# Stick-breaking attention: the transposes of two tiles at every other step, in place of one tile at each

## The chip, the core and the metric

The kernel runs on one NeuronCore of one Trainium2 chip. The metric is the device time of one execution in microseconds. A core has TensorE (PE, with its weight loads shown as PEld), VectorE (DVE), ScalarE (ACT), GpSimd (POOL) and SyncE (SP, which issues the DMAs). Each of them works through its own instructions in the order in which the program gives them, and waits on semaphores for what another engine has to finish first.

## What is computed

One layer (`DEPTH = 1`) over 2048 tokens of width 1024: modulated RMSNorm, a stick-breaking attention with 16 heads of 64, an output projection, and a SwiGLU network of width 2816. Only the attention is touched by the change. Cut to that:

```
z = q k^T * 64**-0.5                       # per head, s_pos < t_pos only
rest = reverse cumulative sum over s of softplus(z)
a = exp(z - rest)                          # 0 where s_pos >= t_pos
o = a v
```

The kernel uses exp(z - rest) = sigmoid(z) times the product of sigmoid(-z) over all later positions. So a row of `a` is a sigmoid times a running product, and the running product is a scan from the right.

## The kernel before

**Units and steps.** The attention is cut into 160 units: 8 pairs of heads (`p`), 4 blocks of 512 queries (`qb`), 2 heads of the pair (`e`), and the blocks of 512 keys from the diagonal one back to the first (`sc`). A unit has four tiles of 128 queries by 512 keys, called rows `r`; on the diagonal row `r` has only `(r + 1) * 128` keys. The main loop (L1020) runs over 640 steps `s` and some more to drain; step `s` begins tile `s`, which is row `s % 4` of unit `s // 4`. Further stages of older tiles are done in the same step, with a delay in steps. All four computing engines take their instructions in the order of the source (`manual_schedule`); nothing is reordered by a planner. This list (L56) is therefore the order of every queue:

```
ORDER_IN_SLOT = [
    ("av", 9), ("score", 0), ("proj", 0), ("turn", 6), ("sig", 0), ("stick", 0), ("high", 6), ("low", 6)
]
```

**The stages.** `score` (L501) is two matmuls into one of two PSUM banks of the pool `zps`. `sig` is two sigmoids on ACT: `a` = sigmoid(z) into SBUF (L518) and sigmoid(-z) back into the same PSUM bank (L520). `stick` is a scan on DVE (L535, on the diagonal L530) that reads that bank, and a product on POOL (L542) that completes the tile of weights `a`. Since a scan is the last reader of its bank, the scores of step `s` can only begin when the scan of step `s - 2` has ended. `turn` (L552) transposes 128 keys of all four rows of a unit, so four transposes on PE (one to four on the diagonal), into one of the two PSUM banks of the pool `tps`. `high` (L562, ACT) and `low` (L568, DVE) split that bank into two tiles of the reduced format fp32r, rounded value and remainder; after `low` the bank is free. `av` (L580) is two matmuls that add the weighed values of those 128 keys.

**The projections beside it.** `proj` puts slices of the coming projections of q, k and v between the others, by `project_to`: about 1.3 slices a step, a slice being three matmuls (`mm3`, L144 to L146), so most steps have one, some two, some none. Where a product is complete, ACT copies it (L404 for k and q, L443 for v) and DVE takes the remainder (L405). For v two slices are left empty (`VGAP = 2`) and then PE turns the copy (L449), which ACT and DVE split again (L453, L454). In the first pair of heads `proj` also turns the normed input (L297, `x_turn`), in the same two banks of `tps`. From step 120 on, at every even step (`LATE_FROM, LATE_STEP = 120, 2`), one piece of the modulation vectors is added up on DVE (L204).

Of the kernel before, what the change touches and what calls it, by code (L numbers as in the profile page):

```python
# [52 lines left out]
    "tmp": 4, "w": 3, "a": 10,  # L53
}

ORDER_IN_SLOT = [  # L56
    ("av", 9), ("score", 0), ("proj", 0), ("turn", 6), ("sig", 0), ("stick", 0), ("high", 6), ("low", 6)
]

LATE_FROM, LATE_STEP = 120, 2  # L60
# [19 lines left out]
def hybrid_trunk_kernel(  # L80
# [401 lines left out]
    def project_to(n):  # L482

        nonlocal done
        while done < min(n, sum(SLICES)):
            next(pending)
            done += 1
        if done == sum(SLICES):
            next(pending, None)
# [425 lines left out]
    def wo_load(half, k2, tag):  # L915
        hl = att.tile([P, 2, 2, BT], F32R, name=f"wo{half}_{k2}", tag=tag, bufs=BUFS[tag])
        nc.sync.dma_start(f32(hl), wo_s[half][:, 2 * k2 : 2 * k2 + 2])
        w_o[half, 2 * k2], w_o[half, 2 * k2 + 1] = hl[:, 0], hl[:, 1]

    def lead_in(first, end):  # L920

        for n in range(first, end + 3):
            if n < end:
                o_load(0, n)
            if first <= n - 2 < end:
                o_add(0, n - 2)
            if first <= n - 3 < end:
                o_prep(0, n - 3)
            yield

    def gate_load(which, tiles):
        for half, sl in enumerate(HALVES):
            tiles.append(att.tile([P, BT], F32, name=f"gate{which}_{half}", tag="w", bufs=BUFS["w"]))
            nc.sync.dma_start(tiles[half], gate_rows[which, :, sl])

    def out_projection(b):


        tiles = [(i, half) for i in range(4) for half in range(2)]
        if b in (0, NB - 1):  # L940
            tiles.sort(key=lambda t: t[1])
        for at, (i, half) in enumerate(tiles):
            y_ps[b, i, half] = bank("x", at % (4 if b else 2), f"y{b}_{i}_{half}")
            for k in range(KC):
                ts = slice(i * P, (i + 1) * P)
                mm3(
                    y_ps[b, i, half], (o_split[b, k][:, 0, ts], o_split[b, k][:, 1, ts]),
                    (w_o[half, k][:, 0], w_o[half, k][:, 1]), k == 0, k == KC - 1,
                )
                tick()  # L950
                beside_out(b, 8 * at + k)
                yield
            after(1, y_square, b, i, half)
            if half == 0:
                continue
            if b == 0:
                after(1, y_gate, i)
            after(2, y_norm, b, i)

            held = LAST_HELD if (b, i) == (NB - 1, 3) else 0  # L960
            after(7 + held, x1_add, b, i)
            after(10 + held, x1_square, b, i)
            after(16 + held, x1_scale, b, i)
        for k in range(KC):
            after(19 + held + H2_STEP * k, h2_turn, b, k)
# [44 lines left out]
        "score": score, "sig": sigmoids, "stick": break_sticks,  # L1010
        "turn": turn, "high": split_high, "low": split_low, "av": weigh_values,
    }
    last = max(d for _, d in ORDER_IN_SLOT)
    weight = 0.0
    wo_weights = split_wo()
    ahead_of_wo = lead_in(0, 6)
# [3 lines left out]
    for s in range(4 * len(units) + last):  # L1020
        if s % 4 == 0 and s // 4 < len(units):
            p, e, qb, sc = units[s // 4]
            at = STEPS.index((p, qb)) if (p, qb) != PARKED else STEPS.index((p, 1)) - 1
            project_to(sum(SLICES[: at + 1]) + 1)
        if s >= LATE_FROM and s % LATE_STEP == 0:
            next(late, None)
        if s >= SPLIT_FROM and s % SPLIT_STEP == 0:
            next(wo_weights, None)
        if s >= lead_from and s % WO_STEP == 0:
            next(ahead_of_wo, None)  # L1030
        if done == sum(SLICES):
            if first_out is None:
                first_out = out_projection(0)
                for k2, tag in enumerate(("ht", "ht", "ht", "ht")):
                    wo_load(1, k2, tag)
                for step in ahead_of_wo:
                    pass
                ahead_of_wo = lead_in(6, KC)
            elif s < 4 * len(units):
                next(ahead_of_wo, None)  # L1040
            if s == 4 * len(units):
                gate_load(0, gate)
            if s >= 4 * len(units) - OUT_BEFORE:
                for _ in range(1 if s < 4 * len(units) else 3):
                    next(first_out, None)
        for stage, delay in ORDER_IN_SLOT:
            if stage == "proj":
                i = min(s // 4, len(units) - 1)
                weight += DIAG_WEIGHT if units[i][2] == units[i][3] else 1.0
                project_to(AHEAD - max(0, EAGER - 1 - s) + weight * RATE)  # L1050
            elif 0 <= s - delay < 4 * len(units):
                stages[stage](*divmod(s - delay, 4))
# [489 lines left out]
```

## Time and profile before

| | us |
|---|---|
| median of 3 runs | 2930.34 |
| lowest, highest | 2928.61, 2930.91 |
| the profiled execution | 2927.62 |
| its span in the profile | 2925.8 |
| PE busy | 2842.0 (97%) |
| DVE busy | 2059.7 (70%) |
| ACT busy | 1651.9 (56%) |
| POOL busy | 1264.7 (43%) |

The span is the profiled execution from its first to its last instruction; 1.8 us of the execution lie outside it. That execution is 2.7 us shorter than the median of the runs. An engine's busy time is the union of its instructions' times; a matmul's end is modelled, so consecutive matmuls overlap in the records and a PE that is shown busy may still have waited for a short while. The attention steps lie between 90 and 1460 us of the span; the output projection and the SwiGLU network follow.

### The profile page before, as it was taken

The numbers are of one execution on the slowest core, as the hardware profiler recorded it, in microseconds if no ns is written. First come the engines' busy times: TensorE is split into PE (matmuls) and PEld (weight loads), VectorE is DVE, ScalarE is ACT, GpSimd is POOL, SyncE is SP. The second block draws the span as 40 slices with busy tenths as digits, with TensorE's granted clock in tenths as the row PEclk, the third lists the DMA queues.
The fourth block names the chain that finished last, engine by engine and source line by source line (L and its number), as shares of the span: only waits on it lengthen the run. The fifth ranks groups of instructions, "written<-read, shape, count | busy, mean of one in ns | idle before, by whom it ended". The sixth has DMA issues, their size and how long they took to land.

```text
span 2925.8 us, 41798 instructions
## 1 busy us (share of the span) xinstructions
PE 2842.0 (97%) x13840; PEld 2323.1 (79%) x13840; DVE 2059.7 (70%) x2828; ACT 1651.9 (56%) x3265; POOL 1264.7 (43%) x2024
## 2 busy tenths in 40 slices
PE   7999999999999999999999999999999999999998
PEld 5788887788877888887887788888778888888886
DVE  5788898888888888889865756555675555233477
ACT  4787877777787777777644533333433333322243
POOL 0465666566575655655410122212222222644454
PEclk9999999999999999999999999999999999999999
DMA  8765647657565545646288644335453335545565
GB/s 298 276 204 168 188 142 229 198 164 232 163 212 195 185 133 169 202 121 229 63 294 294 212 137 152 108 95 158 135 182 103 93 103 170 187 139 154 181 219 179
DMA packets 237481, 516.85 MB, mean 177 GB/s; under 512 B 22224, under 2 KB 108240, under 8 KB 219344
## 3 DMA queue, kind: packets, MB, share of 16 engines
q1 hardware_dynamic: 237264, 514.18, 54.8%
q8 instruction: 109, 1.79, 0.2%
q14 instruction: 108, 0.88, 0.1%
HBM read 346.85 MB, written 118.49 MB: 159 GB/s over the span
## 4 chain that ended last, share of the span: by engine, by line
PE 78%; DVE 8%; issue 4%; ACT 4%; DMA 3%; POOL 2%; SPq 0%; DVEq 0%; POOLq 0%; ACTq 0%
PE s L144 9%; PE s L145 9%; PE s L146 9%; PE z L501 8%; PE o L580 7%; PE t L552 7%; PE pj L144 5%; PE pj L145 5%; PE pj L146 5%; PE o L144 4%; PE o L146 4%; PE o L145 4%; DVE w L535 2%; PE y L144 1%; PE y L146 1%
## 5 line engine op out<-in xcount | busy, mean ns | idle before, releaser
L542 POOL TENSOR_TENSOR a<-a,w 128x512 f32<-128x512 f32 (+3 forms) x640 | 617.7, 965 | 232.9 <-DVE w L535 143.0
L535 DVE TENSOR_TENSOR_SCAN w<-z,c,begin 128x512 f32<-128x512 f32 x384 | 491.1, 1279 | 88.8 <-ACT z L520 65.5
L144 PE MATMUL s<-r,l 128*128 128x512 f32 x1232 | 486.5, 395 | 12.6 <-DVE p L1313 10.2
L145 PE MATMUL s<-r,l 128*128 128x512 f32 x1232 | 483.7, 393 | 0.0
L146 PE MATMUL s<-r,l 128*128 128x512 f32 x1232 | 483.3, 392 | 0.0
L518 ACT ACTIVATE a<-z 128x512 f32<-128x512 f32 (+3 forms) x640 | 344.5, 538 | 145.0 <-PE z L501 121.3
L580 PE MATMUL o<-aT,v 128*128 128x512 f32 (+3 forms) x1280 | 412.4, 403 | 0.0
L562 ACT CAST aT<-t 128x512 fp32r<-128x512 f32 (+3 forms) x640 | 337.9, 528 | 124.6 <-PE t L552 116.6
L568 DVE TENSOR_TENSOR aT<-t,aT 128x512 fp32r<-128x512 f32 (+3 forms) x640 | 376.6, 588 | 26.5 <-ACT aT L562 25.6
L501 PE MATMUL z<-kt,qt 128*128 128x512 f32 (+3 forms) x1280 | 370.1, 370 | 23.9 <-DVE w L535 13.3
L552 PE MATMUL t<-begin,a 128*128 128x128 f32 x2176 | 342.2, 272 | 3.1 <-DVE aT L568 2.7
L520 ACT ACTIVATE z<-z 128x512 f32<-128x512 f32 (+3 forms) x640 | 342.6, 535 | 0.0
L552 PEld LDWEIGHTS t<-begin,a 128*128 128x128 f32 x2176 | 272.9, 140 | 86.9 <-DVE aT L568 6.1
L1321 POOL TENSOR_TENSOR one<-p,p 128x512 f32<-128x512 f32 x44 | 70.8, 1610 | 609.0 <-issue 307.2
L144 PE MATMUL pj<-ht,w 128*128 128x512 f32 x768 | 313.0, 408 | 10.6 <-ACT ht L671 5.7
L145 PE MATMUL pj<-ht,w 128*128 128x512 f32 x768 | 306.1, 399 | 0.4 <-DVE ht L676 0.4
L146 PE MATMUL pj<-ht,w 128*128 128x512 f32 x768 | 304.4, 396 | 0.0
L501 PEld LDWEIGHTS z<-kt,qt 128*128 128x128 f32 x1280 | 225.0, 188 | 86.4 <-DVE w L535 29.3
L144 PEld LDWEIGHTS s<-r,l 128*128 128x128 f32 x1232 | 232.5, 189 | 67.0 <-DVE p L1313 6.3
L146 PEld LDWEIGHTS s<-r,l 128*128 128x128 f32 x1232 | 232.5, 189 | 51.3
L145 PEld LDWEIGHTS s<-r,l 128*128 128x128 f32 x1232 | 232.6, 189 | 50.4 <-issue 0.5
L530 DVE TENSOR_TENSOR_SCAN w<-z,begin 128x128 f32<-128x128 f32 (+3 forms) x256 | 209.7, 819 | 79.8 <-ACT z L520 66.7
(156 smaller groups left out, 4872.5 us busy)
## 6 DMA issues: line engine op xcount, KB each, us to landing
ht<-h_s SPq DMA_DIRECT2D x108, 1024.0 KB, 8.2
wi<-in_win SPq DMA_DIRECT2D x86, 512.0 KB, 4.0
qt<-qn SPq DMA_DIRECT2D x124, 256.0 KB, 4.5
ol_qt<-act_s SPq DMA_DIRECT2D x56, 512.0 KB, 3.7
act_s<-S SPq DMA_DIRECT2D x66, 256.0 KB, 4.0
br<-in_wout SPq DMA_DIRECT2D x66, 256.0 KB, 3.6
h_s<-ht SPq DMA_DIRECT2D x16, 1024.0 KB, 8.3
o_s<-os SPq DMA_DIRECT2D x128, 128.0 KB, 2.4
```

Of the source, the lines that this page charges most:

```text
L144: nc.tensor.matmul(acc, lhs[0], rhs[0], start=first, stop=False, **kw)
L145: nc.tensor.matmul(acc, lhs[0], rhs[1], start=False, stop=False, **kw)
L146: nc.tensor.matmul(acc, lhs[1], rhs[0], start=False, stop=last, **kw)
L501: nc.tensor.matmul(z[:, :n], q[:, e, part, r * P : (r + 1) * P], k[:, e, :n], start=part == 0, stop=part == 1,)
L518: nc.scalar.activation(a[:, :n], z[:, :n], AF.Sigmoid, scale=QK_SCALE)
L520: nc.scalar.activation(z[:, :n], z[:, :n], AF.Sigmoid, scale=-QK_SCALE)
L535: nc.vector.tensor_tensor_scan(rest[:, rev], left[:, rev], begin[:, :BT][:, rev], initial=carries[r], op0=ALU.mult, op1=ALU.bypass,)
L542: nc.gpsimd.tensor_tensor(a[:, :n], a[:, :n], rest[:, 1 : n + 1], op=ALU.mult)
L552: nc.tensor.transpose(pt[:, rb * P : (rb + 1) * P], weighed[i, rb][:, j * P : (j + 1) * P], ident)
L562: nc.scalar.copy(hl[:, 0, t0:], pt[:, t0:])
L568: nc.vector.tensor_tensor(hl[:, 1, t0:], pt[:, t0:], f32(hl[:, 0, t0:]), op=ALU.subtract)
L580: nc.tensor.matmul(acc[:, t0:], lhs, hl[:, part, t0:], start=sc == qb and j == 0 and part == 0, stop=sc == 0 and j == 3 and part == 1,)
```

## The change

The list becomes two lists, one for even and one for odd steps. At an even step `s` the tiles `s - 6` and `s - 5` are both transposed, at an odd step none is. The splits keep their delay of 6, but at an odd step `high` and `low` stand ahead of `sig` and `stick`, so that the second bank of a pair is split in the step after its transposes before that step's sigmoids and scan.

```diff
 ORDER_IN_SLOT = [
-    ("av", 9), ("score", 0), ("proj", 0), ("turn", 6), ("sig", 0), ("stick", 0), ("high", 6), ("low", 6)
+    [("av", 9), ("score", 0), ("proj", 0), ("turn", 6), ("turn", 5),
+     ("sig", 0), ("stick", 0), ("high", 6), ("low", 6)],
+    [("av", 9), ("score", 0), ("proj", 0), ("high", 6), ("low", 6), ("sig", 0), ("stick", 0)],
 ]
...
-    last = max(d for _, d in ORDER_IN_SLOT)
+    last = max(d for order in ORDER_IN_SLOT for _, d in order)
...
-        for stage, delay in ORDER_IN_SLOT:
+        for stage, delay in ORDER_IN_SLOT[s % 2]:
```

## The prediction

> **What bounds it now.** I read the page first, then the stretch of the attention, its waits, and the timelines of single engines. Busy times, and the shares of the chain that ended last:
>
> ```profile
> PE 2842.0 (97%) x13840; PEld 2323.1 (79%) x13840; DVE 2059.7 (70%) x2828; ACT 1651.9 (56%) x3265; POOL 1264.7 (43%) x2024
> PE 78%; DVE 8%; issue 4%; ACT 4%; DMA 3%; POOL 2%; SPq 0%; DVEq 0%; POOLq 0%; ACTq 0%
> ```
>
> TensorE bounds the whole. The stretch of the attention alone:
>
> ```profile
> core 0: us, PE busy (x) PEld busy (x) DVE busy (x) ACT busy (x) POOL busy (x), PEclk, DMA share, GB/s
> 90.00:1460.00 1370.00, 1336.16 (x7223) 1093.46 (x7222) 1164.13 (x1495) 1058.84 (x2190) 822.35 (x1715) 1.00 0.56 181
> ```
>
> DVE is busy 1164.13 of 1370 us (85%), so PE leads by little. The waits there (who waited for whom: us in total, times, longest):
>
> ```profile
> ACT aT L562 <- PE t L552: 116.6, 223, 2.4
> DVE w L530 <- ACT z L520: 66.7, 110, 1.9
> DVE w L535 <- ACT z L520: 65.5, 159, 1.9
> PEld z L501 <- DVE w L535: 29.3, 49, 1.7
> ```
>
> ACT and DVE wait often, PE seldom, and then for a scan that frees a bank of scores. Ends of matmuls being modelled, I counted PE's stalls from starts: a pair of score matmuls that begins later than its predecessor's usual spacing allows. From step 24 on they sum to 38.0 us: 23.8 us in 41 even steps, 14.2 us in 26 odd ones. A change of order can win little more; the matmuls remain. Two steps and a stall, PE first (start, duration):
>
> ```profile
> 1234.26 0.71 PE L580 MATMUL o<-aT,v 128*128 128x512 f32 x2
> 1234.80 0.62 PE L501 MATMUL z<-kt,qt 128*128 128x512 f32 x2
> 1235.26 0.39 PE L144 MATMUL pj<-ht,w 128*128 128x512 f32 x1
> 1235.49 0.40 PE L145 MATMUL pj<-ht,w 128*128 128x512 f32 x1
> 1235.73 0.40 PE L146 MATMUL pj<-ht,w 128*128 128x512 f32 x1
> 1235.96 0.60 PE L552 MATMUL t<-begin,a 128*128 128x128 f32 x4
> 1236.32 0.71 PE L580 MATMUL o<-aT,v 128*128 128x512 f32 x2
> 1236.86 0.63 PE L501 MATMUL z<-kt,qt 128*128 128x512 f32 x2
> 1237.33 0.60 PE L552 MATMUL t<-begin,a 128*128 128x128 f32 x4
> 1237.68 0.71 PE L580 MATMUL o<-aT,v 128*128 128x512 f32 x2
> 1239.18 0.44 PE L501 MATMUL z<-kt,qt 128*128 128x128 f32 x2 [0.79 <-DVE w L535]
> ```
>
> ACT at the same place:
>
> ```profile
> 1236.16 0.59 ACT L443 COPY vT<-pj 128x512 f32<-128x512 f32 x1 [1.04 <-PE pj L146]
> ```
>
> and DVE, in brackets the idle time before an instruction and who ended it:
>
> ```profile
> 1234.65 1.28 DVE L535 TENSOR_TENSOR_SCAN w<-z,c,begin 128x512 f32<-128x512 f32 x1 [0.19 <-ACT z L520]
> 1235.85 0.67 DVE L568 TENSOR_TENSOR aT<-t,aT 128x512 fp32r<-128x512 f32 x1
> 1237.84 1.28 DVE L535 TENSOR_TENSOR_SCAN w<-z,c,begin 128x512 f32<-128x512 f32 x1 [1.33 <-ACT z L520]
> ```
>
> A full step with one slice lasts 2.06 us (1234.26 to 1236.32). In the next one the slice is empty, and the copy of v, which waits on ACT for the product of its own step, has held the sigmoids behind it for 1.04 us; so the scan is late and PE stands.
>
> **The transposes on PE.** No instruction is added or removed. Transposes in a row begin 109 ns apart (807 pairs, 700 to 1400 us). Behind a group, the first `o` begins 28 ns after the last transpose, but the second comes 316 ns later, in place of 233: 28 + 83 = 111, so leaving the transposes costs about nothing. Eight in a row also appear: four `vt` at 101.51, four `xT` at 101.95, 0.44 us for four. Turning eight at once saves 2 ns a pair, 0.6 us in 320 pairs.
>
> The granted clock is 1.00 over the stretch, in which transposes take 0.44 of every 2.06 us. The Trainium skill, "TensorE: Matmul & The Clock Gate" (Part 4: PE-mode transpose), holds that transposes do not count as activity for the clock gate like matmuls do, which speaks against bunching them; by it some windows could lose clock. No run so far shows it.
>
> **The order on ACT and DVE, pair by pair.** From the timelines: a scan ends 3.19 us after its scores begin (1232.74 to 1235.93) and starts 1.91 after; DVE is free for the next instruction 1.20 after a scan's start and 0.60 after a `low`'s. Let an even step's scores begin at 0, full tiles, one slice a step. Before: scan 1.91 to 3.19; `low` from 3.11, DVE free at 3.71; the odd scores begin at 2.06, their scan is ready at 3.97: 0.26 us to spare in every step. Scores two steps on are due at 4.12, the bank was free at 3.24: 0.88 of reserve. After: eight transposes shift the odd scores by 0.36 to 2.42. Scan 1.91 to 3.19, two `low` until 4.31, odd scan ready at 4.33, 0.02 to spare; DVE free at 5.53, the next even scan ready at 6.03, 0.50 to spare. Reserves for the scores: 0.88 and 0.88. So in a regular pair nothing moves. The 116.6 us that ACT waits for transposes may shrink, but no one on the path waits for that.
>
> What changes is where an extra DVE instruction falls.
> - Ahead of an even scan (the pieces of L204, 1.04 us each, are always there) it meets 0.50 of slack in place of 0.26: the scan is 0.24 earlier. Some 15 of the even stalls have it directly ahead: -3.6 us.
> - Ahead of an odd pair (remainders of k, q, v) the slack is 0.02 in place of 0.26. About 8 odd stalls: +1.9 us.
> - The ACT queue of an odd step becomes proj's copy, `high`, sigmoids. Where that copy waits for a matmul of its own step (12 turns of v and 8 product ends fall in odd steps), `high`, which had long been ready, is stuck behind it and the sigmoids come 0.50 later (one `high`). Where the bank's reserve is 0.5 or less, PE pays: 7 such places, at most +3.5 us. Queued behind are the sigmoids, scan and POOL product of that step; the scores two steps on wait.
>
> **The two banks of the transposes.** The second group of a pair needs the bank that the odd step before has already split: some 1.8 us early. In the first pair of heads three even-step groups wait for `low` now (2.7 us); with `low` ahead of the odd scan that wait goes: -2.7. But an `x_turn` at an odd step (four of them) now finds both banks taken and waits for the `low` of the even step before: between 0 and 1.8 us each, I take 2.5 us in all, since light steps are among them. The later uses, `av` three steps behind and POOL's product three steps ahead, keep over 3 us. No DMA moves.
>
> Sum: -3.6 + 1.9 + 3.5 - 2.7 + 2.5 - 0.6 = +1.0 us on 2927.6 for the profiled execution; against the median, which is 2.7 higher, 2931.
>
> **Rivals.**
> - *Slower, the odd scan last in its pair.* Both `low` stand ahead of it, 0.60 more, and only 0.36 is returned by later scores. A scan that is 0.24 later costs some 8 us over the odd steps' reserves (sum of what exceeds each); 0.44 later, 18 us; the full 0.61, 32. It decides once DVE is behind by more than those 0.02 us, which the 85% makes common; against it, a stalled PE gives the next pair its time back. With the ACT queue's 0.50 in addition, about 2945. A rule would have it so: the same page of the Trainium skill (table of the engine's figures) calls ScalarE's queue strictly first in, first out; the trace agrees in the 1.04 us row above.
> - *Faster, the even scan first.* If every even stall shrinks by 0.24 rather than only those behind L204, 41 x 0.24 = 9.8 and the three bank waits 2.7: 2918. At 0.61 each it would be some 18 + 2.7, 2909. For it: even steps hold 23.8 of the 38.0 us. Against: under a DVE backlog the work ahead of an even scan is the same in both orders.
> - *It does not do what it says:* the second group waits for its bank in most pairs, so PE stands with both groups and the order is only a delay. 320 x 0.1 us = 32 us, 2963; the 1.8 us of lead speak against it.
> - *The clock:* if it fell to half for one tenth of the attention, 137 us more. The granted 1.00 with 21% of transposes speaks against it.
>
> **How the numbers follow.** About 0.2% (5.9 us) can be told from no change. No change 0.42; odd scan slower 0.31; banks 0.02; clock 0.01; faster 0.24. The likeliest case's own range is 2925 to 2936. For 8 in 10 the range goes from 2914, most of the faster case, to 2949, the odd scan 0.44 later; about 0.08 lies below and 0.12 above.
>
> **What would show it.** Right: eight `t` in a row 109 ns apart, PE's busy time unchanged in the attention, ACT's wait for `t` below 116.6, stalls of `z` near 38 us with fewer on even steps, odd scans with next to no idle ahead of them. Wrong: the `z` stalls of odd steps well above 14 us (slower), of even steps well below 24 (faster), a wait of `t` for `aT` in most pairs, or a granted clock below 1.00.

## Result: 2925.86 us after, 2930.55 us before

| | before | after |
|---|---|---|
| median of 20 runs, us | 2930.55 | 2925.86 |
| lowest to highest, us | 2927.06 to 2932.63 | 2920.70 to 2927.93 |
| ratio to before, 95% interval | | 0.9984, 0.9977 to 0.9990 |
| profiled execution (its span), us | 2927.62 (2925.8) | 2925.50 (2923.7) |
| span from the first scores to the first product of the SwiGLU network, us | 1528.4 | 1524.7 |

The kernel became 4.7 us faster, 0.16%. The bound of 0.2% that the prediction took for what can be told from no change was too wide: with 20 runs a side the interval is clear of 1. The first scores begin at 93.5 us of the span after and at 91.2 before, a difference of the start that the other profiles show too (91.2 to 95.6 over all kernels); from there on the attention and the output projection take 3.7 us less.

Page and windows of the changed kernel; the columns are those of before:

```profile
PE 2841.5 (97%) x13840; PEld 2339.6 (80%) x13840; DVE 2035.9 (70%) x2828; ACT 1637.6 (56%) x3265; POOL 1269.3 (43%) x2024
PE 81%; DVE 7%; ACT 4%; issue 3%; DMA 3%; POOL 2%; SPq 0%; DVEq 0%; POOLq 0%; ACTq 0%
...
90.00:1460.00 1370.00, 1336.94 (x7238) 1110.72 (x7237) 1145.09 (x1498) 1046.88 (x2196) 827.52 (x1717) 1.00 0.56 182
```

PE's work is the same. DVE's is not: 2035.9 us against 2059.7, 19 us less in the attention alone, with the same 2828 instructions. That is the line to stop at, since nothing was taken from DVE. The waits in the attention:

```profile
DVE w L538 <- ACT z L523: 75.0, 147, 2.0
DVE w L533 <- ACT z L523: 66.6, 105, 1.9
ACT aT L565 <- PE t L555: 66.3, 138, 2.4
...
PEld z L504 <- DVE w L538: 26.4, 43, 1.4
```

ACT's wait for transposes fell from 116.6 to 66.3 us, as expected, and nobody gained by that. PE at the place that the prediction showed (lines are 3 further down in this kernel):

```profile
1234.02 0.63 PE L583 MATMUL o<-aT,v 128*128 128x512 f32 x2
1234.49 0.63 PE L504 MATMUL z<-kt,qt 128*128 128x512 f32 x2
1234.96 0.40 PE L147 MATMUL pj<-ht,w 128*128 128x512 f32 x1
1235.19 0.39 PE L148 MATMUL pj<-ht,w 128*128 128x512 f32 x1
1235.42 0.40 PE L149 MATMUL pj<-ht,w 128*128 128x512 f32 x1
1235.66 1.04 PE L555 MATMUL t<-begin,a 128*128 128x128 f32 x8
1236.45 0.72 PE L583 MATMUL o<-aT,v 128*128 128x512 f32 x2
1237.01 0.62 PE L504 MATMUL z<-kt,qt 128*128 128x512 f32 x2
1237.47 0.63 PE L583 MATMUL o<-aT,v 128*128 128x512 f32 x2
1238.88 0.44 PE L504 MATMUL z<-kt,qt 128*128 128x128 f32 x2 [0.78 <-DVE w L538]
```

Eight transposes in a row take 0.79 us to the next start, 0.36 before for four and 0.43 for the four more: 109 ns each, as worked out. The stall behind the copy of v is still there (0.78 against 0.79).

PE's stalls, counted from starts as in the prediction (delays under 60 ns left out, hence 37.5 for its 38.0):

| us | before | after |
|---|---|---|
| scores, even steps from 24 | 23.4 | 14.5 |
| scores, odd steps from 24 | 14.1 | 13.0 |
| transposes `t`, from step 24 | 1.1 | 7.2 |
| steps 0 to 23: scores; `t`; `xT` | 5.2; 3.5; 2.0 | 5.8; 0.6; 5.5 |
| projections and the rest | 9.5 | 8.6 |
| sum | 58.8 | 55.2 |

Of the 8.9 us that the even steps gained, 7.4 lie in steps 120 to 420 (16.3 to 8.9), where the late modulation is summed.

### The profile page after: what moved, and what is told of

It is laid out like the page before. It is cut to its first block, busy times and chain, and to the rows that moved or that the text cites. A ratio compares the mean times of both kernels' runs of the same rounds, so it can differ in the third digit from the quotient of the medians.

```text
span 2923.7 us, 41817 instructions
## 1 busy us (share of the span) xinstructions
PE 2841.5 (97%) x13840; PEld 2339.6 (80%) x13840; DVE 2035.9 (70%) x2828; ACT 1637.6 (56%) x3265; POOL 1269.3 (43%) x2024
## 4 chain that ended last, share of the span: by engine, by line
PE 81%; DVE 7%; ACT 4%; issue 3%; DMA 3%; POOL 2%; SPq 0%; DVEq 0%; POOLq 0%; ACTq 0%
PE s L147 9%; PE s L148 9%; PE s L149 9%; PE z L504 8%; PE o L583 7%; PE t L555 7%; PE pj L147 5%; PE pj L148 5%; PE pj L149 5%; PE o L148 4%; PE o L147 4%; PE o L149 4%; DVE w L538 2%; PE y L147 1%; PE y L148 1%
## 5 line engine op out<-in xcount | busy, mean ns | idle before, releaser
L583 PE MATMUL o<-aT,v 128*128 128x512 f32 (+3 forms) x1280 | 388.3, 385 | 0.0
L571 DVE TENSOR_TENSOR aT<-t,aT 128x512 fp32r<-128x512 f32 (+3 forms) x640 | 359.7, 596 | 25.3 <-ACT aT L565 24.9
L565 ACT CAST aT<-t 128x512 fp32r<-128x512 f32 (+3 forms) x640 | 313.2, 531 | 76.2 <-PE t L555 66.3
L555 PE MATMUL t<-begin,a 128*128 128x128 f32 x2176 | 292.3, 273 | 5.6 <-DVE aT L571 5.2
L555 PEld LDWEIGHTS t<-begin,a 128*128 128x128 f32 x2176 | 256.1, 140 | 51.3 <-DVE aT L571 6.9
L504 PEld LDWEIGHTS z<-kt,qt 128*128 128x128 f32 x1280 | 225.8, 188 | 77.5 <-DVE w L538 26.4
```

The source lines that it names most:

```text
L504: nc.tensor.matmul(z[:, :n], q[:, e, part, r * P : (r + 1) * P], k[:, e, :n], start=part == 0, stop=part == 1,)
L555: nc.tensor.transpose(pt[:, rb * P : (rb + 1) * P], weighed[i, rb][:, j * P : (j + 1) * P], ident)
L565: nc.scalar.copy(hl[:, 0, t0:], pt[:, t0:])
L571: nc.vector.tensor_tensor(hl[:, 1, t0:], pt[:, t0:], f32(hl[:, 0, t0:]), op=ALU.subtract)
L583: nc.tensor.matmul(acc[:, t0:], lhs, hl[:, part, t0:], start=sc == qb and j == 0 and part == 0, stop=sc == 0 and j == 3 and part == 1,)
```

## Experiments

Ratios are to the kernel before on the same chip. Three questions: which half of the change works, what the pieces of the modulation sums have to do with it, and what holds the transposes up.

### Which half works: pairs alone, early split alone

**x1_pairs_only**

```diff
-    [("av", 9), ("score", 0), ("proj", 0), ("high", 6), ("low", 6), ("sig", 0), ("stick", 0)],
+    [("av", 9), ("score", 0), ("proj", 0), ("sig", 0), ("stick", 0), ("high", 6), ("low", 6)],
```

> Pairs at even steps as in the change, but odd steps keep the old order (sigmoids and scan ahead of high and low). Queue theory: DVE's order is then that of before (scan, low, scan, low), and the second group of a pair waits for a low that comes last in the odd step: odd scores to scan end 3.19 us less 0.08 of overlap, low 0.67, four transposes 0.44, av 0.46 make a loop of about 4.7 us a pair against 4.1 to 4.5 now, so 40 to 170 us slower, about 3000 us, with some 0.2 to 0.5 us of wait of t for aT in most of the 320 pairs. Rival, that the pairing itself is what TensorE gains by (fewer changes between transposes and products): as fast as the changed kernel or faster, 2926 us or less.

Measured: 3057.78 us, 1.0436 (1.0421 to 1.0450), 129 us slower. In the waits of its attention (90 to 1580 us):

```profile
PEld t L555 <- DVE aT L571: 149.7, 181, 2.7
```

The second group of a pair waits for a `low` that comes last in the odd step. So TensorE gains nothing by the pairs as such; they need the split to go ahead.

**x2_lead_only**: one list for all steps.

```diff
+    [("av", 9), ("score", 0), ("proj", 0), ("turn", 5), ("high", 6), ("low", 6), ("sig", 0), ("stick", 0)],
```

> No pairs: one tile is turned at every step, with delay 5, and split a step later ahead of that step's sigmoids and scan (the odd order of the change at all steps). Queue theory: DVE alternates scan and low as before, each scan has the old 0.26 us to spare, so pieces of the modulation sums delay even scans as before: even stalls of z stay near 23 us; the waits of t for a bank (4.6 us before, 7.8 in the changed kernel) go to under 1, and the copies of proj that hold up high and sigmoids act in both parities. Together 2925 to 2933 us, between the two kernels. Rival, that the early split is the gain: 2925 or less with even stalls of 15 us or less. Rival, that the pairing is the gain: 2930 or more.

Measured: 2932.57 us, 1.0010 (1.0002 to 1.0019): inside the range, but not between the two kernels. It is slightly slower than the kernel before, where the second rival had put it. The stalls of scores fell, from 37.5 to 26.4 us, which I had not expected; and the waits of `t`, which I had put under 1 us, rose from 4.6 to 17.7 (steps 0 to 23 included). The early split moves waits from the scores to the transposes. So neither half gains alone. Two things were therefore open: why the scores wait less, and why the transposes wait.

### The pieces of the modulation sums

**x3_after_late_odd** and **x4_before_late_odd**: the same edit in the changed kernel and in the one before.

```diff
-        if s >= LATE_FROM and s % LATE_STEP == 0:
+        if s >= LATE_FROM and s % LATE_STEP == 1:
```

> The changed kernel, with the pieces of the late modulation sums (1.04 us each on DVE) put at odd steps in place of even ones. Queue theory: a piece now stands ahead of two lows and the odd scan, which has 0.02 us to spare in place of 0.50: the gain in steps 120 to 420 is lost, stalls of z there go back from 14.7 us to 20 or more, and the time to 2929 to 2933. Rival, that the gain has nothing to do with these pieces: 2926, stalls unchanged within 2 us.

> The kernel before, with the same pieces at odd steps. Queue theory: all steps have the same 0.26 us there, so the parity is nearly indifferent: within 3 us of the kernel before, 2927.5 to 2933.5. If the parity matters in itself (the pieces collide with other even-step work), it is faster by the 4 to 5 us of the change, 2926.

Measured: x3 2943.72 us, 1.0048 (1.0035 to 1.0061); x4 2937.53, 1.0032 (1.0021 to 1.0042). The gain of the change turned into a loss, by more than I gave it; and the kernel before lost too, which I had excluded. In both, two long waits of a product (`pj`) for its bank, of 1.7 to 2.2 us, came in at steps 173 and 376, with a window of half clock behind each (last section). They came with the new place of the pieces, so the pair is not clean: of x3's 19 us over the changed kernel, and of x4's 9 over the kernel before, some 6 are that. This is an estimate: the two waits, less the 1.4 us that stood at step 376 already, and 1.7 us for each window of 3.4 us at half clock.

**x8_pairs_at_odd**

```diff
-        for stage, delay in ORDER_IN_SLOT[s % 2]:
+        for stage, delay in ORDER_IN_SLOT[(s + 1) % 2]:
```

> The two lists of the change swapped: pairs at odd steps, splits ahead of sigmoids and scan at even ones; the pieces of the modulation sums stay at even steps. Queue theory: they now stand ahead of two lows and a scan with 0.02 us to spare, as in x3, but without a shift of the pieces against the banks of the products, so the loss is 8 to 14 us against the changed kernel, 2934 to 2940. Rival, that pairs gain by themselves: 2926.

Measured: 2943.53 us, 1.0045 (1.0033 to 1.0058), 17 us worse than the changed kernel (each held against the kernel before on its own chip), a little beyond what was expected. The same pairs, at the other parity of the pieces, lose.

**x5_before_short** and **x6_after_short**: the pieces, but for the first of each sum, cut to 8 of their 512 columns, which leaves the sums incomplete.

```diff
-            nc.vector.scalar_tensor_tensor(acc, w[:, i], scale, acc, op0=ALU.mult, op1=ALU.add)
+            nc.vector.scalar_tensor_tensor(acc[:, :8], w[:, i, :8], scale, acc[:, :8], op0=ALU.mult, op1=ALU.add)
```

> The kernel before, with seven of eight pieces of each late modulation sum cut to 8 of their 512 columns (the sums are left incomplete), so that their DVE time drops from about 1.04 to about 0.1 us and nothing is moved. Queue theory: the even stalls behind the pieces go, even z stalls of steps 120 to 420 fall from 16.3 us to about 9, and the time by some 6 to 8 us, to about 2923. Rival, that the even stalls come from elsewhere: under 3 us gained.

> The changed kernel with the same cut. Queue theory: it had won most of its time behind just these pieces, so it gains only 1 to 3 us by the cut, about 2923, and its lead over x5_before_short shrinks from 4.7 us to between -1 and +2. Rival, that its lead has nothing to do with the pieces (pairing or the early split in itself): it stays 4 to 5 us ahead of x5_before_short.

Measured: x5 2918.89 us, 0.9958 (0.9945 to 0.9972); x6 2920.64, 0.9965 (0.9953 to 0.9978). The lead of the change is gone: from the first scores to the first product of the SwiGLU network the profiles have 1524.0 and 1523.9 us, against 1528.4 and 1524.7 with whole pieces. Both gained more than forecast, since 14 of the 56 pieces lie in the SwiGLU network, where the cut takes some 5.5 us off either kernel (1306.2 to 1300.5 us before, 1305.5 to 1300.1 after).

So the change wins behind these pieces. But the prediction's reason, more idle time ahead of the even scan, could not be the whole of it, since the pieces themselves are shorter. The group of L204 in three kernels, the third being x13 below (busy us, mean ns of one, then the idle time before):

```profile
L204 DVE SCALAR_TENSOR_TENSOR aacc<-aw,c_act,aacc 128x512 f32<-128x512 f32 x56 | 58.0, 1036 | 4.1 <-DMA aw<-in_ada_w 3.9
```

```profile
L207 DVE SCALAR_TENSOR_TENSOR aacc<-aw,c_act,aacc 128x512 f32<-128x512 f32 x56 | 42.9, 766 | 4.2 <-DMA aw<-in_ada_w 4.1
```

```profile
L204 DVE SCALAR_TENSOR_TENSOR aacc<-aw,c_act,aacc 128x512 f32<-128x512 f32 x56 | 45.6, 815 | 4.5 <-DMA aw<-in_ada_w 4.3
```

What differs is the instruction ahead. DVE and then POOL in the kernel before:

```profile
599.63 0.67 DVE L568 TENSOR_TENSOR aT<-t,aT 128x512 fp32r<-128x512 f32 x1
600.21 1.34 DVE L204 SCALAR_TENSOR_TENSOR aacc<-aw,c_act,aacc 128x512 f32<-128x512 f32 x1
601.47 1.27 DVE L535 TENSOR_TENSOR_SCAN w<-z,c,begin 128x512 f32<-128x512 f32 x1
```

```profile
599.91 1.09 POOL L542 TENSOR_TENSOR a<-a,w 128x512 f32<-128x512 f32 x1
```

and in the changed one:

```profile
602.92 1.28 DVE L538 TENSOR_TENSOR_SCAN w<-z,c,begin 128x512 f32<-128x512 f32 x1
604.11 0.73 DVE L207 SCALAR_TENSOR_TENSOR aacc<-aw,c_act,aacc 128x512 f32<-128x512 f32 x1
604.75 1.28 DVE L538 TENSOR_TENSOR_SCAN w<-z,c,begin 128x512 f32<-128x512 f32 x1
```

```profile
604.26 0.63 POOL L544 COPY c<-w 128x1 f32<-128x1 f32 x1 [1.61 <-DVE w L538]
604.84 1.09 POOL L545 TENSOR_TENSOR a<-a,w 128x512 f32<-128x512 f32 x1
```

Before, the piece comes behind a `low`; by then POOL has begun the product that the last scan released, and the piece, which reads two tiles from SBUF as the product does, takes 1.34 us and ends 0.55 us behind that product. After, two scans follow each other across the step's border, so the piece comes directly behind a scan, before POOL has been told of it. It takes 0.73, and now POOL waits: its copy of one column takes 0.63 in place of 0.18. Over the 48 pieces in the attention (both instructions of L202 and L204): with a two-input instruction of POOL under way at their start (in the kernel before 34 times L542's product) 35 pieces of 1240 ns on average, without one 13 of 680, in the kernel before; 6 of 1032 and 42 of 690 in the changed one; 52.2 us in all against 35.2.

That the piece is held, and not slowed, shows in single pieces and in x5. In the attention of the kernel before, 30 pieces of L204 begin well inside a product of L542 (over 150 ns before its end); they last 833 to 1493 ns, and every one ends 546 to 549 ns behind the product. The seven that begin while POOL is idle last 736 to 744. In x5 a piece has 8 columns in place of 512, and 28 such pieces that begin inside a product still last 335 to 991 ns and end 20 to 25 ns behind it; so x5 shortened its pieces by much less than I had expected. All 56 in the kernel before, in x5 and in x6 (ns at the least, in the median and at the most):

```profile
L204 DVE SCALAR_TENSOR_TENSOR aacc<-aw,c_act,aacc x56: 735/875/1493, 370.0 to 2156.6; 128x512 f32<-128x512 f32 x56
```

```profile
L204 DVE SCALAR_TENSOR_TENSOR aacc<-aw,c_act,aacc x56: 209/381/991, 373.8 to 2151.6; 128x8 f32<-128x8 f32 x56
```

```profile
L207 DVE SCALAR_TENSOR_TENSOR aacc<-aw,c_act,aacc x56: 198/203/711, 375.9 to 2151.4; 128x8 f32<-128x8 f32 x56
```

The first piece of a sum (L202) reads one tile from SBUF, and in the kernel before it is held too: three that begin inside a product take 1019 to 1206 ns, two that begin while POOL is idle 476 and 478. The Trainium skill, "SBUF — State Buffer" (Who interferes with whom), has the rule: a VectorE instruction with two inputs in SBUF and a GpSimd instruction that reads SBUF share one port pair, and whichever starts first holds it for its whole length. The trace agrees in both directions: the pieces of L204 are held as above, and the 11 products of L542 that begin during a piece take 1.60 us (median) in place of 1.09.

**x13_before_piece_behind_scan** and **x14_after_piece_behind_scan** part that from the idle time. The piece is held back until behind the scan of its own step; nothing else moves.

```diff
+    held, holding = [], [False]
...
-                ada_add(acc, loaded[at], k0, i, k0 + i == 0)
+                piece = (acc, loaded[at], k0, i, k0 + i == 0)
+                held.append(piece) if holding[0] else ada_add(*piece)
...
+            holding[0] = True
             next(late, None)
+            holding[0] = False
...
+            if stage == "stick":
+                while held:
+                    ada_add(*held.pop(0))
```

> The kernel before; each piece of the late modulation sums goes on DVE directly behind its step's scan instead of ahead of it (behind a low); nothing else moves. Port theory: the pieces lasted 1088 ns on average in the attention behind a low, with POOL's product L542 under way at the start of 35 of 48, and 733 ns in the changed kernel, where they come directly behind a scan, before the product starts; so here too they fall to 700 to 780 ns, DVE saves some 16 us, z stalls of steps 120 to 420 fall from 21.4 us to about 15, and the time by 4 to 7 us, to 2923 to 2926, without any pairs. Theory of the prediction (idle time to spare ahead of the scan): all scans have the same 0.26 us to spare in this kernel, so nothing is gained, 2929 to 2931.

> The changed kernel with the pieces directly behind the even scan, so ahead of two lows and the odd scan. Port theory: they stay short, 700 to 780 ns, so most of the gain stays: 2925 to 2929. Theory of the prediction: the odd scan has 0.02 us to spare and each piece now delays it by its full length, as in x3 and x8, so the gain is lost and more: 2934 to 2944.

Measured: x13 2925.74 us, 0.9989 (0.9980 to 0.9998); x14 2926.45, 0.9989 (0.9980 to 0.9998). Without any pairs, x13 gets most of the gain of the change by the place of the pieces alone (0.11 of 0.16%, with intervals that overlap): they fall to 815 ns (I had given 700 to 780), and even stalls of steps 120 to 420 from 16.3 to 8.7 us, as in the changed kernel (8.9). x14 has the pieces where by the prediction's reason they should hurt most, ahead of the odd scan with 0.02 us to spare, and keeps most of the gain; the odd stalls of scores from step 24 stay at 13.1 us, and the waits of `t` rise only from 7.2 to 9.2. So the idle-time theory falls. The port theory holds, with a correction: x14's pieces did not stay as short as I had forecast. They take 885 ns on average in the attention, since at the start of 21 of the 48 POOL was still at an earlier product (1082 ns; the other 27 took 732). To stand behind a scan is not enough; POOL must be free as well.

The theory also reads x3 and x8: there the pieces stand behind a `low` again, 1251 and 1124 ns on average in the attention; and x2, whose pieces stand behind scans, 754 ns, and whose scores waited less. On DVE x8 has scan, `low`, piece, `low`, scan and x14 scan, piece, `low`, `low`, scan, and by their ratios they lie some 16 us apart. The longer pieces make some 11 us of that (an estimate, 0.24 us on each of 48); the rest is not parted.

### What holds the transposes up

The waits of `t` that came in with the change are nearly all for the second group of a pair. PE at step 164, with ACT and DVE, in the changed kernel:

```profile
448.52 0.62 PE L555 MATMUL t<-begin,a 128*128 128x128 f32 x4
449.94 0.66 PE L555 MATMUL t<-begin,a 128*128 128x128 f32 x4 [0.79 <-DVE aT L571]
```

```profile
448.08 0.59 ACT L446 COPY vT<-pj 128x512 f32<-128x512 f32 x1 [1.48 <-PE pj L149]
448.56 0.59 ACT L565 CAST aT<-t 128x512 fp32r<-128x512 f32 x1
```

```profile
449.19 0.69 DVE L571 TENSOR_TENSOR aT<-t,aT 128x512 fp32r<-128x512 f32 x1 [1.72 <-ACT aT L565]
```

The copy of v waits 1.48 us for the product of its own step, `high` stands behind it though its tile was turned long ago, `low` behind `high`, and the second four transposes behind `low`.

**x7_split_ahead_of_proj**, and **x10_only_high_ahead** with `("high", 6), ("proj", 0), ("low", 6)` at that place:

```diff
-    [("av", 9), ("score", 0), ("proj", 0), ("high", 6), ("low", 6), ("sig", 0), ("stick", 0)],
+    [("av", 9), ("score", 0), ("high", 6), ("low", 6), ("proj", 0), ("sig", 0), ("stick", 0)],
```

> The changed kernel with high and low of the odd step ahead of proj as well (av, score, high, low, proj, sig, stick). Queue theory: a copy of proj that waits for a product of its own step no longer holds up high, and a remainder of proj on DVE no longer holds up the low that frees a bank; waits of t behind step 24 fall from 7.2 us to 4 or less, odd z stalls from 12.9 by up to 3, and the time to 2921 to 2924, if the kernel before is at 2930.5. If the copies and remainders of proj are not what makes the second group wait, 2925 to 2927 as in the changed kernel.

> As x7_split_ahead_of_proj, but at odd steps only high goes ahead of proj; low stays behind it (av, score, high, proj, low, sig, stick). It parts the two things that x7 did: if the copies of proj on ACT were what held up the bank, it is as fast as x7, 2922; if the remainders of proj on DVE ahead of low were, it stays with the changed kernel, 2926. I expect the first for the most part, 2922 to 2924, since a copy that waits for its own step's product holds high, and low with it, for up to 1 us, and a remainder lasts 0.6.

> The changed kernel once more, beside the following ones on one chip, so that they can be held against it and not only against the kernel before: 0.998 to 0.999 of the kernel before.

> x7_split_ahead_of_proj once more, beside x13 and x14: 0.996 to 0.998 of the kernel before. If x13 reaches 2924 or less, its lead over x13 tells what the pairs and the early split are worth beside the shorter pieces: 1 to 4 us.

Measured: x7 2921.90 us, 0.9969 (0.9957 to 0.9980), and again as x15 2922.53, 0.9977 (0.9968 to 0.9985); x10 2921.91, 0.9977 (0.9968 to 0.9986), beside the changed kernel as x9 with 2924.51, 0.9984 (0.9975 to 0.9993). At the same place x7 has:

```profile
444.95 1.06 PE L555 MATMUL t<-begin,a 128*128 128x128 f32 x8
445.76 0.71 PE L583 MATMUL o<-aT,v 128*128 128x512 f32 x2
447.46 0.51 PE L504 MATMUL z<-kt,qt 128*128 128x256 f32 x2 [0.99 <-DVE w L533]
```

```profile
442.45 1.07 ACT L565 CAST aT<-t 128x512 fp32r<-128x512 f32 x2 [0.20 <-PE t L555]
444.51 0.59 ACT L446 COPY vT<-pj 128x512 f32<-128x512 f32 x1 [0.99 <-PE pj L149]
```

Both splits go ahead of the copy and all eight transposes run through. Half of the wait comes back at once, since the sigmoids still stand behind the copy: the scores at 447.46 us wait 0.99 us, and in the changed kernel, at 451.53, 0.47. From the first transpose to these scores it is 2.51 us in x7 and 3.01 in the changed kernel. The waits of `t` from step 24 are 3.8 us in x7 and 5.5 in x10, against 7.2; from the first scores to the first product of the SwiGLU network both have 1520.4 us, against 1524.7. So by the time the copies on ACT are most of it, 2.6 us of x10's lead over x9 on one chip; by the waits of `t` they are half (1.7 of 3.4 us). Whether `low` ahead of the remainders adds anything to the time is not settled, the intervals overlap; those of x10 and x9 overlap too. The odd stalls of scores hardly changed (13.6 and 12.0), which I had given up to 3 us. x7 and x10 are the fastest kernels with whole pieces, 7 to 9 us ahead of the kernel before.

**x11_sig_ahead_of_proj** goes on in that direction, **x12_before_sig_ahead_of_proj** does it without pairs.

```diff
+    [("av", 9), ("score", 0), ("sig", 0), ("stick", 0), ("proj", 0), ("turn", 6), ("turn", 5),
+     ("high", 6), ("low", 6)],
+    [("av", 9), ("score", 0), ("high", 6), ("low", 6), ("sig", 0), ("stick", 0), ("proj", 0)],
```

> Pairs as in x7, and at both parities sigmoids and scan go ahead of proj too (even: av, score, sig, stick, proj, turn, turn, high, low; odd: av, score, high, low, sig, stick, proj). Queue theory: no copy of proj can hold up sigmoids, so stalls like the one at 1239.18 us of the kernel before (about 1 us each, five to eight of them) go, z stalls fall below 22 us from 28; the copies come some 1 us later, which the second bank of the products mostly covers: 2914 to 2921. Rival: the later copies and remainders make the products wait for their banks, pj stalls rise by as much, 2922 or more.

> The kernel before (one tile turned at every step), with sigmoids and scan ahead of proj at every step. It tells whether what x11 gains needs the pairs: by the queue theory the same stalls behind copies go, 2920 to 2926, still behind x11 by 3 to 6 us, since the pieces of the modulation sums stay ahead of every even scan with 0.26 us to spare.

Measured: x11 2924.81 us, 0.9987 (0.9978 to 0.9996); x12 2933.82, 1.0014 (1.0005 to 1.0023). Both miss their forecast. The stalls of scores fell as forecast, to 19.7 us from step 24 in x11, but the later copies cost it again, in part as the rival had it. PE's waits of x11 from 160 to 1460 us:

```profile
PE vt L452 <- ACT vT L446: 8.1, 12, 1.1
PE z L504 <- DVE w L538: 6.7, 18, 0.9
PE pj L147 <- DVE qn L408: 2.5, 1, 2.5
...
PE pj L147 <- DVE kn L408: 2.2, 1, 2.2
```

The copy of v, now behind the sigmoids, comes too late for its own turning, which waited 0.7 us in the kernel before in all and waits 8.1 now. The two single waits of a product, 2.5 and 2.2 us, each have a window of half clock behind them (last section), which neither I nor the rival had counted. In x12 the turnings of v wait 5.4 us, and one product waits 3.6 us for a load (`ht<-h_s`).

## Why the prediction was wrong

- *The transposes on PE, zero:* right. Spacing, busy time and the granted clock of 1.00 are unchanged. By the rule of the Trainium skill that the prediction named ("TensorE: Matmul & The Clock Gate", Part 4: PE-mode transpose) some windows could have lost clock; in the attention of the changed kernel, with eight in a row, none did.
- *A regular pair moves nothing:* not contradicted. With the pieces cut, the two kernels take 1524.0 and 1523.9 us over the attention and output projection. One figure in it was misread: four more transposes shift the odd scores not by 0.36 us but by four times 109 ns, 0.44 (by 0.46 in the rows above, 1234.49 to 1237.01 us against 2.06). That leaves about 0.1 us to spare ahead of the odd scan and 0.4 ahead of the even one, in place of 0.02 and 0.50, and makes the next term smaller still.
- *An extra DVE instruction ahead of an even scan, -3.6 us:* this is the step that failed. The stalls fell by 8.9. The sign was right and the reason was not: I took the piece as 1.04 us in both kernels and priced only 0.24 us of idle time ahead of it. The order changed the piece itself, 1036 to 766 ns, because it now starts ahead of POOL's product and is not held by it; x13 gets most of the gain by that alone, and x14 shows that the idle time hardly mattered. The spread was to be read before: the trace of before gives these 56 instructions of one shape 735 ns at the least, 875 in the median and 1493 at the most (the first of the three lines shown with the pieces), which for one form on one engine asks what the others were doing.
- *Ahead of an odd pair, +1.9:* not seen. Odd stalls of scores went from 14.1 to 13.0.
- *`high` behind proj's copy, at most +3.5:* right that `high` is stuck behind the copy, wrong in what then waits. It showed as waits of the second group for its bank, not as late scores: x7 takes 3.4 us of them away, and x7 and x10 got some 3 to 4 us back.
- *The two banks, 1.8 us early and so nothing:* wrong as a term of its own. Waits of `t` from step 24 rose by 6.1 us, because that lead was worked out for a step without a waiting copy. This is the same cost as in the line above; the prediction had +3.5 for both together. Of the 3.8 us that stay in x7, 2.4 lie at steps 586 and 612, where instructions of the output projection stand ahead of `low` on DVE; the prediction had not counted those either.
- *The first pair of heads:* `t` -2.7 forecast and -2.9 measured; `x_turn` at odd steps +2.5 forecast and +3.5 measured.

Put together, the forecast sum of +1.0 should have been about -3.6 by these counts (by chance the size of the one term that failed). The measured time lies inside the stated range, and even inside the likeliest case's own; that is owed to luck, since the even stalls fell by 5.3 us more than forecast and the waits of `t` took part of it back. The faster rival had the right place, even steps, with 9.8 us for them, but the same wrong reason, and no price for the bank waits that took most of it back (+6.1). The slower rival, the odd scan last in its pair, did not happen here; x3 and x8 lost, but through longer pieces and through the banks.

## What to carry to other kernels

When an order is changed, look at which instructions of two engines will now start side by side, not only at who waits for whom: an instruction's duration in the trace is that of its neighbourhood, and a wide spread for one shape says so. A two-input VectorE instruction between SBUF tiles is best issued directly behind the instruction that will release GpSimd's work, before that work starts and while GpSimd has no earlier work under way (x14). GpSimd's work then waits in its place; here POOL, busy for 43% of the span, had room for that. And where a queue is strictly in order, anything that is ready belongs ahead of a copy that waits for the present step, up to the point where the copy's own reader is next.

## What the runs showed that was not expected

A pause of TensorE of about 2 us can cost clock behind it. In x4 a product waited for its bank; PE, then the windows around it:

```profile
467.56 0.50 PE L144 MATMUL pj<-ht,w 128*128 128x512 f32 x1 [2.12 <-DVE gr L264]
...
468.79 0.63 PE L145 MATMUL pj<-ht,w 128*128 128x512 f32 x1
```

```profile
464.00:468.30 4.30, 2.05 (x8) 1.09 (x8) 4.06 (x7) 2.96 (x7) 3.97 (x7) 1.00 0.47 139
468.30:471.70 3.40, 3.40 (x10) 2.76 (x10) 2.15 (x4) 0.31 (x2) 1.32 (x3) 0.51 0.94 299
```

The granted clock halves for 3.4 us and the products start 0.43 us apart in place of 0.23. The four pauses of 1.7 to 2.2 us in x3 and x4 each had such a window behind them, and so had those of 2.5 and 2.2 us in x11; pauses of up to 1.5 us in the attention of the kernels before and after had none. The length of the pause alone does not decide it. x1 had ten of 1.8 to 2.5 us and two windows, and one of 2.5 us in x12 and one of 1.7 in x14 had none behind them. In x8, on the other hand, a window (1394.8 to 1398.2 us, granted clock 0.50) follows 3.4 us in which no wait of TensorE was longer than 0.81 us; it was shown busy for 2.27 of them, transposes among its work. What cost the clock there no run settles. So a wait of about 2 us can cost up to 1.7 us more than itself (an estimate: 3.4 us at half clock), but not every time. The Trainium skill, "TensorE: Matmul & The Clock Gate" (Why this matters for your kernels), asks for no gaps of TensorE over some 3 us; here gaps of two thirds of that were enough.
